# First scale and shift by matmul, constant-tile matmuls, and issue edges round the heads of the first layer

## The chip, the cores and the metric

One core of a Trainium2 chip. The metric is the device time of one launch in microseconds (us), lower is better. Engines: TensorE (PE, with its weight loads as PEld), VectorE (DVE), ScalarE (ACT), GpSimd (POOL), SyncE (SP, which here only issues loads). Each engine works through its own instructions strictly in order.

## The reference, cut to what matters

Four layers over T = 512 rows of width D = 1024: gated linear attention (GLA), a gated convolution MLP, a retention layer, a latent attention layer. The change lies in the first, GLA:

```
cs = silu(c)
shift, scale, gate = split(cs @ mod_w + mod_b, 3)       # 1024 each
h = x * (1 + scale) + shift
q, k, v, r, a = split(h @ gla_w_in)    # 4 heads: q, k 128 wide, v, r 256 wide; a 16 wide
log_a = log_sigmoid(a @ w_a2 + b_a) / 16;  bcum = cumsum(log_a) by chunk
q_dec = q * 128**-0.5 * exp(bcum);  k_inv = k * exp(-bcum)
att = tril(q_dec @ k_inv.T)
o = att @ v + q_dec @ S;  S = S * decay + k_dec.T @ v   # S carried from chunk to chunk
y = (rms_norm(o) * silu(r)) @ gla_w_o
```

## The kernel before, in words

All products run in a form of float32 that TensorE takes in one pass after rounding. To keep the precision each operand is split into a rounded part (`hi`, a cast on ScalarE) and its rest (`lo`, a subtraction on VectorE), and `mm3` does three matmuls: hi by hi, hi by lo, lo by hi (L154 to L156). So every weight tile goes through a load into `raw` (four buffers), a cast (L114) and a subtraction (L115) into `wsp`.

`gla_start` walks the eight 128-row blocks k of the contraction. For each it loads 1 MB of modulation weights (`ms`, in two halves), the block of x transposed (`xq`) and 512 KB of weights (`raw`). VectorE multiplies each `ms` half by the broadcast silu(c) (`csr`) and sums the row (L508): this is scale and shift for the block. ScalarE applies them (L516, into `hT` and `xv`), and 24 matmuls of 512 columns follow, into eight accumulators: v of the first two heads, and q and k of heads 0 and 1.

Then come, on TensorE: 16 matmuls for `a` (L574), the projection r of heads 0 and 1 with the four decay-log matmuls (L601) inside, the transposes of small vectors (L342), then the heads. For each head `gla_prep` makes `qd` and `ki`; `gla_inner` does q by k (12 matmuls of 128 columns), transposes k, splits it into `kt` (L114, L115), masks (`af`), and builds the carried state `sf` by chunk; `gla_outer` gives the output. Between the heads lie the projections q, k of heads 2 and 3 (`gla_qk`), after them v of heads 2 and 3 (`gla_v`), the transposes of the gated output (`gate_T`, L442, split by L117 and L118 into `uT`) and r of heads 2 and 3.

All PSUM banks that are not accumulators come from one pool called `aux`; a matmul into one waits for the readers of what was there. The modulation for the next layer is made by VectorE in sixteen 1024-wide products (L411) of `rawm` tiles, which share the four `raw` buffers. `PLACE` says how many pairs of them are written at each of seven places; a scheduler then interleaves the streams of each engine by its own estimate of when each instruction can start. So the order in the source is not the order on an engine.

Of the kernel before, what the change touches and what calls it, by code (L numbers as in the profile page):

```python
# [67 lines left out]
def layouts(ins):  # L68


    w = ins["gla_w_in"][0]

    def mod(i):
        m, b = ins["mod_w"][0, i], ins["mod_b"][0, i]
        both = np.concatenate([m[:, 1024:2048].T, m[:, 0:1024].T], 1)
        bias = np.stack([b[1024:2048].reshape(8, P), b[0:1024].reshape(8, P)], -1)
        return np.ascontiguousarray(both), np.ascontiguousarray(bias.transpose(1, 0, 2).reshape(P, 16))

    m0, m1 = mod(0), mod(1)
    return {"l_ba": np.ascontiguousarray(ins["gla_b_a"][0].reshape(4, P).T),  # L80
            "l_x": np.ascontiguousarray(ins["x"][0].T),
            "l_mod": m0[0], "l_modb": m0[1], "l_mod1": m1[0], "l_modb1": m1[1],
            "l_c": np.ascontiguousarray(ins["c"].reshape(8, P).T),
            "l_w": np.ascontiguousarray(np.concatenate([w[:, 1024:1536], w[:, 0:256], w[:, 512:768]], 1))}


# [10 lines left out]
class Kern:  # L97
# [125 lines left out]
    def small(self, n, name, dt=F32):  # L223
        return self.tiny.tile([P, 8], dt, tag=name, name=name)[:, :n]

    def rsqrt(self, v):

        nc, n = self.nc, v.shape[1]
        y, t, h = self.small(n, "rs_y"), self.small(n, "rs_t"), self.small(n, "rs_h")
        i = self.small(n, "rs_i", I32)  # L230
        nc.vector.tensor_scalar(i, v.bitcast(I32), 1, None, op0=OP.logical_shift_right)
        nc.vector.tensor_scalar(y.bitcast(I32), i, -1, 0x5F3759DF, op0=OP.mult, op1=OP.add)
        nc.vector.tensor_scalar_mul(h, v, -0.5)
        for _ in range(3):
# [75 lines left out]
    def setup_late(self, ph):  # L310

        nc, a = self.nc, self.a
        self.cs = self.cons.tile([P, 8], F32, name="cs")
        nc.sync.dma_start(self.cs, a["l_c"])
        nc.scalar.activation(self.cs, self.cs, AF.Silu)

    def vectors(self, ph):

# [63 lines left out]
    def gla(self):  # L382
        nc, a, tc = self.nc, self.a, self.tc
        w = a["gla_w_in"][0]
        with ExitStack() as ctx:
# [4 lines left out]
            with tc.tile_pool(name="gla_in", bufs=1, reuse_waits="tile") as ph:  # L390
# [9 lines left out]
                order = list(range(8)) + [(0, 2048), (0, 2560)]  # L400

                def place(where):
                    for _ in range(self.PLACE[where]):
# [12 lines left out]
                decay = self.gla_decay(ph, out, arow)  # L416
                place(0)
                self.gla_r(xT, 0, lambda b, ps: nc.scalar.activation(u[0][:, b, :], ps, AF.Silu))
                place(1)
                self.vectors(ph)  # L420
                tril = out.tile([P, P], F32, name="tril")
                nc.sync.dma_start(tril, a["k_tril"])
                place(2)
            with tc.tile_pool(name="gla_core", bufs=1, reuse_waits="tile") as ph:
# [59 lines left out]
    def gla_start(self, ph, out):  # L484
# [2 lines left out]
        nc, a = self.nc, self.a  # L487
        tl, xT = self.new_hT()
        accs = [self.acc() for _ in range(8)]
        mb = ph.tile([P, 8, 2], F32, name="mb")  # L490
        nc.sync.dma_start(mb, a["l_modb"].rearrange("p (k j) -> p k j", j=2))
        xs = [self.main.tile([P, 2, T], F32, tag=f"res{q}", name=f"xq{q}") for q in range(4)]

        def loads(k):
            r = slice(k * P, k * P + P)
            m = ph.tile([P, 2, D], F32, tag="ms", name="ms", bufs=4)
# [24 lines left out]
            self.split(sp[:, 0], sp[:, 1], raw)  # L521
            return sp

        for k in range(8):
            m, raw = loads(k)
            operand(k, m)
            sp = weights(raw)
            wv = [sp[:, i, 0:512] for i in range(2)]
            for b in range(NB):
                self.mm3(accs[b], [t[:, b * P:(b + 1) * P] for t in xT.k[k]], wv, k == 0, k == 7)  # L530
            for j in range(4):
                self.mm3(accs[4 + j], [sp[:, i, 512 + j * P:640 + j * P] for i in range(2)], xT.k[k], k == 0, k == 7)
# [4 lines left out]
        for h in range(2):  # L537
# [4 lines left out]
        self.setup_late(ph)  # L542
        return xT, v, raws

    def gla_v(self, out, xT, pr):
# [35 lines left out]
    def gla_decay(self, ph, out, a3):  # L581
# [4 lines left out]
        w3, wh, wl, keep = wr[:96, 0], wr[:96, 1], wf[:96, 0], wf[:, 1]  # L586
# [10 lines left out]
        la = ph.tile([P, 4, T], F32, tag="ms", name="la", bufs=self.MS)  # L597
        e = ph.tile([P, 4, T], F32, tag="ms", name="lz", bufs=self.MS)
        for h in range(4):
            pz = self.aux()  # L600
            nc.tensor.matmul(pz, w3[:, h * P:(h + 1) * P], a3, start=True, stop=True)  # L601
            nc.scalar.activation(e[:, h], pz, AF.Abs, bias=ba[:, h:h + 1])
            nc.vector.tensor_scalar(la[:, h], pz, ba[:, h:h + 1], 0.0, op0=OP.add, op1=OP.min)
        nc.scalar.activation(e, e, AF.Exp, scale=-1.0)
        nc.scalar.activation(e, e, AF.Ln, bias=1.0)
        decay = []
        for h in range(4):
            nc.vector.tensor_sub(la[:, h], la[:, h], e[:, h])
            c = ph.tile([P, T], F32, tag="t2", name="cum", bufs=2)
            nc.vector.tensor_tensor_scan(c, keep, la[:, h], 0.0, op0=OP.mult, op1=OP.add)  # L610

            em = self.small(4, "em")
            nc.scalar.activation(em, c[:, 63:T:P], AF.Exp, scale=1.0 / 16)
            d = e[:, h].rearrange("p (b i) -> p b i", b=NB)
            c3 = c.rearrange("p (b i) -> p b i", b=NB)
            nc.vector.tensor_sub(d, c3, c3[:, :, 63:64].to_broadcast([P, NB, P]))
            e1 = out.tile([P, T], F32, name=f"ep{h}")
            e2 = out.tile([P, T], F32, name=f"em{h}")
            nc.scalar.activation(e1, e[:, h], AF.Exp, scale=1.0 / 16)
            nc.scalar.activation(e2, e[:, h], AF.Exp, scale=-1.0 / 16)  # L620

            dk = out.tile([P, 4], F32, name=f"dk{h}")
            nc.vector.tensor_mul(dk[:, 0:3], e1[:, 127:384:P], em[:, 1:4])
            decay.append((e1, e2, dk))
        return decay

    def gla_prep(self, ph, decay, raw):

# [11 lines left out]
    def gla_inner(self, ph, prep, v, tril):  # L640
# [18 lines left out]
        st, sf = [], ph.tile([P, 256], F32, tag="sf", name="sf")  # L659
# [650 lines left out]
```

## Time and profile before

| | |
|---|---|
| time, median of 3 runs (lowest to highest) | 1259.92 us (1258.68 to 1263.08) |
| the profiled execution | 1261.78 us, of which span 1260.0 us |
| TensorE busy | 1225.5 us (97%) |
| VectorE, ScalarE busy | 817.6 us (65%), 535.3 us (42%) |
| mean granted clock of TensorE | 0.994 |
| read from memory | 141.09 MB |

The span is the stretch from the first to the last recorded instruction; the time of a launch has about 1.8 us round it. The granted clock is the share of full speed that TensorE was allowed: 1.00 is 2.4 GHz, 0.50 is 1.2 GHz.

### The profile page before, as it was taken

Reading aid. Unit: us, or ns where it says so; the run is one execution under the profiler, and the core shown is the slowest. Engines: PE = TensorE matmul, PEld = TensorE weight load, DVE = VectorE, ACT = ScalarE, POOL = GpSimd, SP = SyncE. Lnnn points to the kernel's source line nnn. Section 1 sums busy time; section 2 is a strip of 40 time slices with the busy share of each in tenths; the row PEclk is TensorE's granted clock in tenths of the full one; section 3 lists DMA queues with packets and bytes.
Section 4 is the critical chain, followed back from the end, with each engine's and each line's share of the span. In section 5 each row is a group of like instructions: output and inputs, shape, how many; then the busy total and the mean of one; then the engine's idle time right before and its main releaser. Section 6 shows DMA issues by size and latency. Waiting matters only on the chain.

```text
span 1260.0 us, 16047 instructions
## 1 busy us (share of the span) xinstructions
PE 1225.5 (97%) x5982; PEld 1024.9 (81%) x5982; DVE 817.6 (65%) x1836; ACT 535.3 (42%) x946; POOL 3.7 (0%) x15
## 2 busy tenths in 40 slices
PE   5989999999999999999999999999999999999997
PEld 4767877898888888888788888888888888888886
DVE  5698877788442354445875649556454689687755
ACT  3583444533332223341543333433434347577631
POOL 0000000000000000000000000000000000000000
PEclk9998999999999999999999999999999999999999
DMA  9658554147322333333152332323332333212221
GB/s 346 213 171 258 168 195 134 51 125 226 97 90 98 101 99 89 97 134 117 66 158 86 88 90 82 92 85 92 117 106 96 109 98 107 69 50 78 84 84 68
DMA packets 133043, 148.44 MB, mean 118 GB/s; under 512 B 9825, under 2 KB 92152, under 8 KB 132964
## 3 DMA queue, kind: packets, MB, share of 16 engines
q1 hardware_dynamic: 132964, 147.40, 36.5%
q8 instruction: 47, 0.77, 0.3%
q14 instruction: 32, 0.26, 0.1%
HBM read 141.09 MB, written 6.29 MB: 117 GB/s over the span
## 4 chain that ended last, share of the span: by engine, by line
PE 86%; DVE 7%; ACT 4%; DMA 2%; issue 2%; SPq 0%; DVEq 0%; ACTq 0%
PE acc L154 25%; PE acc L156 25%; PE acc L155 25%; PE po L154 1%; PE po L156 1%; PE po L155 1%; PE aux L154 1%; PE aux L156 1%; PE aux L155 1%; DMA raw<-in_gla_w_in 1%; DVE wsp L115 1%; PE aux L899 1%; DMA ms<-in_l_mod 1%; ACT wsp L114 1%; PE aux L1251 1%
## 5 line engine op out<-in xcount | busy, mean ns | idle before, releaser
L115 DVE TENSOR_TENSOR wsp<-raw,wsp 128x1024 fp32r<-128x1024 f32 (+1 forms) x162 | 195.5, 1208 | 192.4 <-ACT wsp L114 192.1
L114 ACT CAST wsp<-raw 128x1024 fp32r<-128x1024 f32 (+1 forms) x162 | 167.9, 1039 | 289.5 <-PE acc L156 253.6
L154 PE MATMUL acc<-hT,wsp 128*128 128x512 f32 (+1 forms) x640 | 244.8, 382 | 0.5 <-DVE v L115 0.5
L156 PE MATMUL acc<-hT,wsp 128*128 128x512 f32 (+1 forms) x640 | 243.7, 381 | 0.0
L155 PE MATMUL acc<-hT,wsp 128*128 128x512 f32 (+1 forms) x640 | 243.3, 380 | 0.0
L154 PE MATMUL acc<-wsp,hT 128*128 128x512 f32 (+2 forms) x448 | 170.0, 386 | 14.6 <-ACT wsp L114 14.6
L155 PE MATMUL acc<-wsp,hT 128*128 128x512 f32 (+2 forms) x448 | 171.6, 383 | 0.0
L156 PE MATMUL acc<-wsp,hT 128*128 128x512 f32 (+2 forms) x448 | 170.3, 382 | 0.0
L154 PEld LDWEIGHTS acc<-hT,wsp 128*128 128x128 f32 x640 | 121.2, 189 | 23.7 <-DVE v L115 1.4
L155 PEld LDWEIGHTS acc<-hT,wsp 128*128 128x128 f32 x640 | 120.9, 189 | 22.1 <-issue 0.2
L156 PEld LDWEIGHTS acc<-hT,wsp 128*128 128x128 f32 x640 | 120.8, 189 | 22.0
L154 PEld LDWEIGHTS acc<-wsp,hT 128*128 128x128 f32 x448 | 84.7, 189 | 29.9 <-ACT wsp L114 14.6
L156 PEld LDWEIGHTS acc<-wsp,hT 128*128 128x128 f32 x448 | 84.6, 189 | 15.1
L155 PEld LDWEIGHTS acc<-wsp,hT 128*128 128x128 f32 x448 | 84.7, 189 | 14.4 <-DVE wsp L115 0.3
L154 PE MATMUL acc<-wsp,uT 128*128 128x512 f32 (+1 forms) x192 | 75.3, 392 | 0.0
L156 PE MATMUL acc<-wsp,uT 128*128 128x512 f32 (+1 forms) x192 | 75.2, 392 | 0.0
L155 PE MATMUL acc<-wsp,uT 128*128 128x512 f32 (+1 forms) x192 | 74.9, 390 | 0.0
L154 PE MATMUL acc<-wsp,p 128*128 128x512 f32 x144 | 56.9, 395 | 0.0
L155 PE MATMUL acc<-wsp,p 128*128 128x512 f32 x144 | 56.9, 395 | 0.0
L156 PE MATMUL acc<-wsp,p 128*128 128x512 f32 x144 | 56.9, 395 | 0.0
L801 DVE SCALAR_TENSOR_TENSOR cv<-acc,cols,cv 128x511 f32<-128x511 f32 x22 | 16.5, 749 | 57.7 <-ACT cv L800 57.7
L800 ACT ACTIVATE cv<-acc,cols 128x512 f32<-128x512 f32 x22 | 17.2, 780 | 82.4 <-PE acc L156 82.4
(357 smaller groups left out, 2062.1 us busy)
## 6 DMA issues: line engine op xcount, KB each, us to landing
raw<-in_w_in_a SPq DMA_DIRECT2D x48, 512.0 KB
raw<-in_ffn_w_up SPq DMA_DIRECT2D x44, 512.0 KB
raw<-in_ffn_w_down SPq DMA_DIRECT2D x22, 512.0 KB
ms<-in_l_mod SPq DMA_DIRECT2D x16, 512.0 KB
raw<-in_gla_w_in SPq DMA_DIRECT2D x16, 512.0 KB
rawm<-in_l_mod SPq DMA_DIRECT2D x16, 512.0 KB
rawm<-in_mod_w SPq DMA_DIRECT2D x16, 512.0 KB
raw<-in_w_out_a SPq DMA_DIRECT2D x16, 512.0 KB
```

The lines of the kernel that those rows point to most:

```text
L114: nc.scalar.copy(hi, src)
L115: nc.vector.tensor_sub(lo, src, self.f(hi))
L154: mm(out, l[0], r[0], start=first, stop=False)
L155: mm(out, l[0], r[1], start=False, stop=False)
L156: mm(out, l[1], r[0], start=False, stop=last)
L800: nc.scalar.activation(t, p, AF.Identity, scale=cw[2 * NT + j], bias=cb[j])
L801: nc.vector.scalar_tensor_tensor(t[:, 1:], p[:, :T - 1], cw[NT + j], t[:, 1:], op0=OP.mult, op1=OP.add)
L899: nc.tensor.transpose(pu[:, b * P:(b + 1) * P], u[:, b, i * P:(i + 1) * P], self.ident)
L1251: nc.tensor.matmul(sc[:, :n], qrT[i][:, s], kr[i][:, :n], start=False, stop=i == 1)
```

## The change

In `gla_start` a new function `first` does block k = 0; the loop does k = 1 to 7 as before. The 1 MB of modulation columns for block 0 comes in a layout of its own (`l_f0`, 256 KB in each of four loads), and scale and shift are 16 matmuls of one column each on TensorE (L546), against silu(c) as eight columns, which one transpose of the small tile `cb` gives. `busy` issues matmuls on a constant tile between them. The load of `csr` moves behind those of block 0. The 24 matmuls of block 0 run with all hi-by-hi products first.

Round the heads: r of heads 0 and 1 is cut after 24 matmuls, where the decay logs stand now; the sums of the decays are made for heads 0 and 1 first (`gla_sums`), for heads 2 and 3 behind head 0; the exponentials run in halves; the state update is one scaled copy on ScalarE and one fused operation on VectorE, rather than an addition and a product on VectorE. `after(engine)` ties what is traced inside it behind the last instruction of that engine, on that engine. `PLACE` changes, and the products of the last three places are tied behind VectorE's last instruction.

```
-    PLACE = (0, 2, 0, 2, 2, 2, 2)
+    WARM = (3, 1, 4, 6)
+    PLACE = (0, 2, 0, 0, 3, 3, 2)
+    def after(self, engine):
+        ins = next(i for i in reversed(self.nc.cur_bb.bb.instructions) if i.engine == engine.engine)
+        return self.tc.issue_after(ins)
...
                 def place(where):
+                    if where > 2:
+                        with self.after(nc.vector):
+                            return place_now(where)
+                    place_now(where)
...
-                decay = self.gla_decay(ph, out, arow)
+                self.vectors(ph)
+                accs = [self.acc() for _ in range(NB)]
+                self.proj_t(xT, self.wsubs(wi, 2048, 2560, 0, 2), 512, None, accs=accs)
+                with self.after(nc.tensor):
+                    logs = self.gla_decay(ph, out, arow)
+                with tc.high_priority():
+                    decay = [self.gla_sums(ph, out, logs, h) for h in range(2)]
                 place(0)
-                self.gla_r(xT, 0, lambda b, ps: nc.scalar.activation(u[0][:, b, :], ps, AF.Silu))
+                self.proj_t(xT, ((k + 2, t) for k, t in self.wsubs(wi, 2048, 2560, 2, 8)), 512,
+                            lambda b, ps: nc.scalar.activation(u[0][:, b, :], ps, AF.Silu), accs=accs)
                 place(1)
-                self.vectors(ph)
...
-                p0 = prep(0)
-                p1 = prep(1)
-                place(3)
-                i0 = self.gla_inner(ph, p0, vh(0), tril)
+                with tc.high_priority():
+                    p0, p1 = prep(0), prep(1)
+                with self.after(nc.tensor):
+                    i0 = self.gla_inner(ph, p0, vh(0), tril)
+                with self.after(nc.scalar), self.after(nc.vector):
+                    decay += [self.gla_sums(ph, out, logs, h) for h in range(2, 4)]
+                    place(3)
...
+            busy(self.WARM[0])
+            with self.after(nc.tensor):
+                nc.tensor.transpose(pt, cb, self.ident[:24, :24])
+                nc.scalar.activation(self.cs, pt[:, 0:8], AF.Silu)
+                nc.vector.tensor_copy(mb.rearrange("p k j -> p (k j)"), pt[:, 8:24])
+            for k in range(8):
+                with self.after(nc.tensor):
+                    if k % 2 == 0:
+                        busy(self.WARM[1 if k else 2])
+                with self.after(nc.tensor):
+                    for j in range(2):
+                        nc.tensor.matmul(pm[j], m[:, k, j], self.cs[:, k:k + 1], start=k == 0, stop=k == 7)
+            with self.after(nc.tensor):
+                busy(self.WARM[3])
...
             if b > 0:
-                nc.vector.tensor_add(sf, pS, sf)
-            nc.vector.tensor_scalar_mul(sf, sf if b else pS, dk[:, b:b + 1])
+                sd = ph.tile([P, 256], F32, tag="sf", name="sd", bufs=3)
+                nc.scalar.activation(sd, sf, AF.Copy, scale=dk[:, b:b + 1])
+                sf = ph.tile([P, 256], F32, tag="sf", name="sf", bufs=3)
+                nc.vector.scalar_tensor_tensor(sf, pS, dk[:, b:b + 1], sd, op0=OP.mult, op1=OP.add)
+            else:
+                nc.vector.tensor_scalar_mul(sf, pS, dk[:, 0:1])
```

The order on the engines follows from the scheduler, so it is shown at three places. First TensorE at the start of the program; `warm` is the constant tile, `m` the modulation columns of block 0. Before:

```order
L154 MATMUL acc<-wsp,hT 128x512 x4
L154 MATMUL acc<-hT,wsp 128x512
L155 MATMUL acc<-wsp,hT 128x512
L156 MATMUL acc<-wsp,hT 128x512
L155 MATMUL acc<-wsp,hT 128x512
```

Now:

```order
L513 MATMUL acc<-warm 128x512 x3
L537 MATMUL acc<-ident,cb 128x24
L513 MATMUL acc<-warm 128x512 x4
L546 MATMUL acc<-cs,m_106 128x1 x4
L513 MATMUL acc<-warm 128x512
L546 MATMUL acc<-cs,m_106 128x1 x4
L513 MATMUL acc<-warm 128x512
L546 MATMUL acc<-cs,m_106 128x1 x4
L513 MATMUL acc<-warm 128x512
L546 MATMUL acc<-cs,m_106 128x1 x4
L513 MATMUL acc<-warm 128x512 x6
L571 MATMUL acc<-wsp,hT 128x512 x4
```

Sixteen constant-tile matmuls, a transpose and 16 one-column matmuls stand ahead of the first product of block 0.

Second ScalarE between `qd` of head 0 and `kt` of head 0; `u` is silu of r. Before:

```order
L418 ACT_TABLE_LOAD
L418 ACTIVATE u_465<-acc 128x512 x4
L114 CAST qd<-qk_449 128x512
L114 CAST ki<-qk_449 128x512
L114 CAST qd<-qk_452 128x512
L114 CAST ki<-qk_452 128x512
L114 CAST kt<-aux 128x384
```

Now:

```order
L116 CAST qd<-qk_491 128x512
L116 CAST ki<-qk_491 128x512
L707 ACTIVATE em_606<-em_606 128x512
L116 CAST qd<-qk_494 128x512
L433 ACT_TABLE_LOAD
L433 ACTIVATE u_504<-acc 128x512
L116 CAST ki<-qk_494 128x512
L433 ACTIVATE u_504<-acc 128x512 x3
L116 CAST wsp<-raw 128x1024 x2
L116 CAST kt<-aux 128x384
```

`qd` and `ki` of head 0 moved ahead of the table load and of `u`; `kt`, which stood behind four casts of 512 columns, stands behind these and two weight casts.

Third VectorE from the split of v of heads 2 and 3 to `kt` of head 2; L417 is the product that was L411, L120 the split of `uT` that was L118. Before:

```order
L115 TENSOR_TENSOR v<-acc,v 128x512
L118 SCALAR_TENSOR_TENSOR uT_73<-aux,cols_714,uT_73 128x512 x4
L115 TENSOR_TENSOR wsp<-raw,wsp 128x1024
L657 TENSOR_TENSOR af<-aux,tril 128x512
L115 TENSOR_TENSOR kt<-aux,kt 128x384
```

Now:

```order
L417 SCALAR_TENSOR_TENSOR rawm,mc_501<-rawm,csr 128x1024 x4
L120 SCALAR_TENSOR_TENSOR uT_73<-aux,cols_533,uT_73 128x512
L417 SCALAR_TENSOR_TENSOR rawm,mc_501<-rawm,csr 128x1024 x2
L120 SCALAR_TENSOR_TENSOR uT_73<-aux,cols_533,uT_73 128x512 x3
L117 TENSOR_TENSOR kt<-aux,kt 128x384
```

Four products stand between the last split of v (just ahead of this piece) and the first of `uT`, and two more behind it. The last two take buffers that the first two give back.

## Rows read from the trace of the kernel before

**Rows 1.** The page, its part on engines: busy us (share of the span) and number of instructions.

```profile
PE 1225.5 (97%) x5982; PEld 1024.9 (81%) x5982; DVE 817.6 (65%) x1836; ACT 535.3 (42%) x946; POOL 3.7 (0%) x15
```

**Rows 2.** The waits of the matmul engine in the first 250 us: who waits, tile and line, for which engine's instruction; us in total, times, longest.

```profile
PE acc L154 <- ACT wsp L114: 14.6, 1, 14.6
PE aux L154 <- ACT ki L114: 4.2, 1, 4.2
PE aux L154 <- ACT kt L114: 2.6, 1, 2.6
PE aux L154 <- DVE sf L665: 0.7, 1, 0.7
...
PE aux L154 <- DVE af L657: 0.5, 1, 0.5
PE aux L601 <- DVE a L578: 0.4, 1, 0.4
```

**Rows 3.** The timeline of all engines at the start: start us, duration us, engine, line, operation, out<-in, in brackets the idle time ahead and what ended it. SPq is SyncE's queue, which issues the loads.

```profile
9.21 1.23 DVE L508 SCALAR_TENSOR_TENSOR ms<-ms,csr 128x1024 f32<-128x1024 f32 x1 [9.21 <-DMA ms<-in_l_mod]
...
12.06 0.81 ACT L516 ACTIVATE hT<-xq,mc 128x512 fp32r<-128x512 f32 x1 [5.59 <-DVE mc L511]
...
13.48 1.03 ACT L114 CAST wsp<-raw 128x1024 fp32r<-128x1024 f32 x1
...
14.56 2.08 PE L154 MATMUL acc<-wsp,hT 128*128 128x512 f32 x4 [14.56 <-ACT wsp L114]
```

**Rows 4.** The timeline of the matmul engine over the first k steps. One matmul is 512 columns wide; the starts tell the pace.

```profile
16.87 0.63 PE L155 MATMUL acc<-wsp,hT 128*128 128x512 f32 x1
17.29 0.63 PE L156 MATMUL acc<-wsp,hT 128*128 128x512 f32 x1
...
20.00 0.39 PE L156 MATMUL acc<-hT,wsp 128*128 128x512 f32 x1
20.23 0.39 PE L154 MATMUL acc<-hT,wsp 128*128 128x512 f32 x1
...
22.27 1.07 PE L154 MATMUL acc<-wsp,hT 128*128 128x512 f32 x4
...
27.71 1.07 PE L154 MATMUL acc<-wsp,hT 128*128 128x512 f32 x4
```

**Rows 5.** One-microsecond stretches of the start: bounds, length, busy us (count) of PE, PEld, DVE, ACT, POOL, granted clock, busy share of the transfer engines, GB/s.

```profile
3.00:4.00 1.00, 0.00 (x0) 0.00 (x0) 0.00 (x0) 0.00 (x0) 0.00 (x0) 1.00 0.82 152
...
10.00:11.00 1.00, 0.00 (x0) 0.00 (x0) 0.96 (x4) 0.00 (x0) 0.00 (x0) 1.00 1.05 426
```

**Rows 6.** The timeline of ScalarE between the decay logs and head 0.

```profile
67.47 2.42 ACT L602 ACTIVATE lz<-aux,ba 128x512 f32<-128x512 f32 x4 [0.80 <-PE aux L601]
69.91 1.28 ACT L604 ACT_TABLE_LOAD   x1
...
74.44 1.92 ACT L605 ACTIVATE lz<-lz 128x2048 f32<-128x2048 f32 x1
...
87.56 1.28 ACT L418 ACT_TABLE_LOAD   x1
88.86 2.06 ACT L418 ACTIVATE u<-acc 128x512 f32<-128x512 f32 x4
...
91.29 0.65 ACT L114 CAST ki<-qk 128x512 fp32r<-128x512 f32 x1
```

**Rows 7.** The timeline of VectorE over the same stretch.

```profile
77.60 2.33 DVE L610 TENSOR_TENSOR_SCAN cum<-wf,la 128x512 f32<-128x512 f32 x2
...
84.65 1.27 DVE L616 TENSOR_TENSOR lz<-cum 128x512 f32<-128x512 f32 x2
...
88.39 1.22 DVE L411 SCALAR_TENSOR_TENSOR rawm<-rawm,csr 128x1024 f32<-128x1024 f32 x1
```

**Rows 8.** The timeline of the matmul engine: its first matmul on head 0 and its first state product of head 1.

```profile
91.99 0.48 PE L154 MATMUL aux<-qd,ki 128*128 128x128 f32 x1 [4.15 <-ACT ki L114]
...
114.35 0.38 PE L154 MATMUL aux<-v,kt 128*128 128x256 f32 x1 [2.55 <-ACT kt L114]
```

**Rows 9.** One-microsecond stretches behind these two waits, columns as in rows 5.

```profile
96.00:97.00 1.00, 1.00 (x5) 0.93 (x5) 0.81 (x2) 0.66 (x1) 0.00 (x0) 0.50 1.15 359
97.00:98.00 1.00, 1.00 (x7) 0.97 (x6) 0.52 (x2) 0.62 (x1) 0.00 (x0) 0.68 0.99 367
...
114.00:115.00 1.00, 0.65 (x4) 0.66 (x5) 1.00 (x3) 1.00 (x3) 0.00 (x0) 0.86 0.97 346
...
117.00:118.00 1.00, 1.00 (x4) 0.81 (x4) 1.00 (x2) 0.41 (x1) 0.00 (x0) 0.50 0.86 303
```

**Rows 10.** The timeline of the matmul engine from the end of the second v projection.

```profile
153.87 0.39 PE L156 MATMUL acc<-wsp,hT 128*128 128x512 f32 x1
154.10 1.91 PE L442 MATMUL aux<-ident,u 128*128 128x128 f32 x16
...
156.50 0.33 PE L154 MATMUL aux<-qd,ki 128*128 128x128 f32 x1
...
158.98 0.39 PE L154 MATMUL aux<-v,kt 128*128 128x256 f32 x1
```

**Rows 11.** The timeline of VectorE over the same stretch.

```profile
155.10 0.69 DVE L115 TENSOR_TENSOR v<-acc,v 128x512 fp32r<-128x512 f32 x1
155.70 2.72 DVE L118 SCALAR_TENSOR_TENSOR uT<-aux,cols,uT 128x512 fp32r<-128x512 f32 x4
```

More of the change, by code (lines that the diff above doesn't have):

```diff
@@ L297, in setup @@
         nc, a = self.nc, self.a
-        cr = a["c"][0]
         self.csr = self.mod.tile([P, D], F32, name="csr")
-        nc.sync.dma_start(self.csr, bass.AP(tensor=cr.tensor, offset=cr.offset, ap=[[0, P], [1, D]]))
-        nc.scalar.activation(self.csr, self.csr, AF.Silu)
+        self.cs = self.cons.tile([P, 8], F32, name="cs")
         self.ident = self.cons.tile([P, P], F32, name="ident")
@@ L308, in setup @@
         self.col = {}
[L310 to L315, printed above, removed]
     def vectors(self, ph):
@@ L489, in gla_start, with busy, first @@
         accs = [self.acc() for _ in range(8)]
+        warm = ph.tile([P, T], F32R, tag="t2", name="warm", bufs=2)
+        nc.vector.tensor_copy(warm, self.ones[:, 0:1].to_broadcast([P, T]))
+        def busy(n):
+            for _ in range(n):
+                nc.tensor.matmul(accs[7], warm[:, :P], warm, start=True, stop=True)
         mb = ph.tile([P, 8, 2], F32, name="mb")
-        nc.sync.dma_start(mb, a["l_modb"].rearrange("p (k j) -> p k j", j=2))
         xs = [self.main.tile([P, 2, T], F32, tag=f"res{q}", name=f"xq{q}") for q in range(4)]
+        def first():
+            cb = ph.tile([24, P], F32, name="cb")
+            nc.scalar.dma_start(cb, a["l_cb"])
+            m = ph.tile([P, 8, 2, P], F32, tag="ms", name="m0", bufs=self.MS)
+            f0 = a["l_f0"].rearrange("p (k j f) -> p k j f", k=8, j=2)
+            raw = self.main.tile([P, self.WN], F32, tag="raw", name="raw", bufs=self.RAW)
+            for k in range(0, 8, 2):
+                nc.sync.dma_start(m[:, k:k + 2], f0[:, k:k + 2])
+            nc.sync.dma_start(xs[0][:, 0], a["l_x"][0:P])
+            halves = [slice(0, 512), slice(512, D)]
+            for h in halves:
+                nc.sync.dma_start(raw[:, h], a["l_w"][0:P, h])
+            cr = a["c"][0]
+            nc.sync.dma_start(self.csr, bass.AP(tensor=cr.tensor, offset=cr.offset, ap=[[0, P], [1, D]]))
+            pt = accs[4][:, 0:24]
+            pm = [accs[6 - j][:, 0:1] for j in range(2)]
+            busy(self.WARM[0])
[12 more added lines that the diff above has]
+                busy(self.WARM[3])
+            mc = self.small(2, "mc")
+            nc.vector.tensor_scalar(mc[:, 0:1], pm[0], mb[:, 0, 0:1], 1.0, op0=OP.add, op1=OP.add)
+            nc.vector.tensor_add(mc[:, 1:2], pm[1], mb[:, 0, 1:2])
+            hi, lo = tl[0][:, 0, 0, :], tl[0][:, 1, 0, :]
+            sp = self.main.tile([P, 2, self.WN], F32R, tag="wsp", name="wsp", bufs=self.WSP)
+            v = ph.tile([P, T], F32, tag="t2", name="xv", bufs=2)
+            with self.after(nc.scalar):
+                for h in halves:
+                    nc.scalar.copy(sp[:, 0, h], raw[:, h])
+            with self.after(nc.scalar):
+                nc.scalar.activation(hi, xs[0][:, 0], AF.Identity, scale=mc[:, 0:1], bias=mc[:, 1:2])
+                nc.scalar.activation(v, xs[0][:, 0], AF.Identity, scale=mc[:, 0:1], bias=mc[:, 1:2])
+            with self.after(nc.vector):
+                for h in halves:
+                    nc.vector.tensor_sub(sp[:, 1, h], raw[:, h], self.f(sp[:, 0, h]))
+                nc.vector.tensor_sub(lo, v, self.f(hi))
+            parts = [([t[:, b * P:(b + 1) * P] for t in xT.k[0]], [sp[:, i, 0:512] for i in range(2)]) for b in range(NB)]
+            parts += [([sp[:, i, 512 + j * P:640 + j * P] for i in range(2)], xT.k[0]) for j in range(4)]
+            order = [[(0, 0), (0, 1), (1, 0)]] * NB + [[(0, 0), (1, 0), (0, 1)]] * 4
+            with self.after(nc.tensor):
+                for t in range(3):
+                    for acc, (l, r), o in zip(accs, parts, order):
+                        nc.tensor.matmul(acc, l[o[t][0]], r[o[t][1]], start=t == 0, stop=False)
@@ L522, in weights @@
             return sp
-        for k in range(8):
+        first()
+        with self.after(nc.scalar):
+            nc.scalar.activation(self.csr, self.csr, AF.Silu)
+        for k in range(1, 8):
             m, raw = loads(k)
@@ L585, in gla_decay @@
         wf = ph.tile([P, 4, T], F32, tag="ms", name="wf", bufs=self.MS)
-        w3, wh, wl, keep = wr[:96, 0], wr[:96, 1], wf[:96, 0], wf[:, 1]
+        keep = out.tile([P, T], F32, name="keep")
+        w3, wh, wl = wr[:96, 0], wr[:96, 1], wf[:96, 0]
         for i in range(6):
@@ L596, in gla_decay @@
         nc.gpsimd.memset(keep[:, 0:T:P], 0.0)
-        la = ph.tile([P, 4, T], F32, tag="ms", name="la", bufs=self.MS)
-        e = ph.tile([P, 4, T], F32, tag="ms", name="lz", bufs=self.MS)
+        la, e = ([out.tile([P, 2, T], F32, name=f"{n}{i}") for i in range(2)] for n in ("ep", "em"))
         for h in range(4):
@@ L601, in gla_decay @@
             nc.tensor.matmul(pz, w3[:, h * P:(h + 1) * P], a3, start=True, stop=True)
[L602 to L624, printed above, removed]
@@ L625, in gla_decay, with gla_sums @@
-        return decay
+            nc.scalar.activation(e[h // 2][:, h % 2], pz, AF.Abs, bias=ba[:, h:h + 1])
+            nc.vector.tensor_scalar(la[h // 2][:, h % 2], pz, ba[:, h:h + 1], 0.0, op0=OP.add, op1=OP.min)
+        for t in e:
+            nc.scalar.activation(t, t, AF.Exp, scale=-1.0)
+        for t in e:
+            nc.scalar.activation(t, t, AF.Ln, bias=1.0)
+        return keep, la, e
+    def gla_sums(self, ph, out, logs, h):
+        nc = self.nc
+        keep, la, e = logs
+        la, e = la[h // 2][:, h % 2], e[h // 2][:, h % 2]
+        nc.vector.tensor_sub(la, la, e)
+        c = ph.tile([P, T], F32, tag="t2", name="cum", bufs=2)
+        nc.vector.tensor_tensor_scan(c, keep, la, 0.0, op0=OP.mult, op1=OP.add)
+        em = self.small(4, "em")
+        nc.scalar.activation(em, c[:, 63:T:P], AF.Exp, scale=1.0 / 16)
+        d = e.rearrange("p (b i) -> p b i", b=NB)
+        c3 = c.rearrange("p (b i) -> p b i", b=NB)
+        nc.vector.tensor_sub(d, c3, c3[:, :, 63:64].to_broadcast([P, NB, P]))
+        nc.scalar.activation(la, e, AF.Exp, scale=1.0 / 16)
+        nc.scalar.activation(e, e, AF.Exp, scale=-1.0 / 16)
+        dk = out.tile([P, 4], F32, name=f"dk{h}")
+        nc.vector.tensor_mul(dk[:, 0:3], la[:, 127:384:P], em[:, 1:4])
+        return la, e, dk
@@ L658, in gla_inner @@
         self.split(at[:, 0], at[:, 1], af)
-        st, sf = [], ph.tile([P, 256], F32, tag="sf", name="sf")
+        st, sf = [], ph.tile([P, 256], F32, tag="sf", name="sf", bufs=3)
         for b in range(3):
```

15 lines of the change are left out of this document (9 added, 6 removed).

## The prediction

> **What bounds the kernel now.** I read the page first: TensorE is busy 1225.5 of 1260.0 us [rows 1], so a gain can only come from its 34 idle microseconds, or from stretches in which it runs at its lower clock. The waits of TensorE say where the idle time is [rows 2]: 14.6 us ahead of the first matmul, then 4.2 us for `ki` of head 0, 2.6 us for `kt` of head 1, and 0.7, 0.5 and 0.4 us. All of it lies in the first 170 us. Behind that TensorE has work all the time, so what is saved or lost round the heads goes to the end unchanged. Third come the timelines and clock of these places.
>
> The start. The first matmul is at 14.56, behind a chain of load (9.21), two products and sums on VectorE, scale (12.06) and cast (13.48, 1.03 long) [rows 3]. The matmuls then start 0.42 us apart, later 0.227 us [rows 4]: the first ones run at half the pace. Block k = 1 starts at 22.27 and block 2 at 27.71, 5.44 us for 24 matmuls [rows 4].
>
> Head 0. TensorE waits 4.15 us, to 91.99 [rows 8], and then runs at a granted clock of 0.50, the 1.2 GHz level, up to the stretch 97 to 98 [rows 9]. Some 5.7 us at half pace lose 2.85, so this place costs 7.0. Head 1 in the same way: 2.55 of waiting to 114.35 [rows 8] and half pace from late in 114 to 115 through 117 to 118 [rows 9], 3.3 us, which lose 1.65: together 4.2. With the 0.44 in front of the decay logs these three cost 11.7.
>
> **The change part by part.** *The start.* TensorE gets sixteen constant-tile matmuls and 16 one-column matmuls, all before 12 us, when it had nothing to do; VectorE loses two 1.2 us products. Block 0 needs f0, x and weights, 1.8 MB, which lie ahead of `csr` in the new queue. But block 1 still needs `csr` and its own `ms`, x and weights, and the bytes ahead of its weights are the same 4.2 MB as before. So the place to look at is the landing of the weights of block 1, not block 0. From the landing of the first `ms` half at 9.21 [rows 3], 3.15 MB remain to them; at 410 GB/s, a little under the settled rate [rows 5], that is 7.7 us: 16.9. Early on the rate falls to 152 GB/s for some microseconds [rows 5]; if that came from the small scattered load `mb`, which now is a small one of another shape, they land up to 2 us earlier, at 14.9. I take 16.2. Behind them in the new order come the cast (1.03), `hT` and `xv` (0.75 each), and on VectorE the `lo` of the weights, a product for block 2 (1.15) and the `lo` of `hT` (0.6): 3.9 us, so the eighth matmul of block 1 starts at 20.1 and 17 more at 0.227 end it at 24.0. Before it was 27.71: 3.7 us gained. Ends: 2.8 (late landing, part of block 0 at half pace) to 5.0 (landing at 14.9). Behind it TensorE is the slowest again: 5.44 us a block, against 1.83 MB or 4.5 us of loads, so the gain stays.
>
> *Heads 0 and 1.* The logs start 24 matmuls into r, not 10, so 3.2 us later; the 0.44 wait goes, as `a` is ready. The chain behind them is shorter. Before: four Abs (2.42), table, Exp (1.92 with its table 3.2), Ln (1.92), then sums for four heads, two scan pairs of 2.33 and so on [rows 6, 7], three products of 1.15 from 88.39 ahead of the splits [rows 7], and the table and `u` ahead of `qd` and `ki` on ScalarE [rows 6]. Now only heads 0 and 1 stand in it: one scan pair and one pair of offsets (1.27) go, so do the three products but one, and 3.3 us of table and `u`. I walk it in the old clock: Abs from 69.9 to 72.4, Exp to 75.7, Ln of the first half to 77.9, differences and scans to 81.5, offsets to 82.7, one product to 83.8, `ki` and its `lo` to 87.0. TensorE is through with r and the vectors at 87.1. So the 4.15 us wait shrinks to 0.1.
>
> But `kt` is late next. On ScalarE between `ki` and `kt` of head 0 now stand the table load (1.28), four `u` (2.06), casts of head 1 and two weight casts of 1.03: from 86.0 to 92.9, and `kt` is there at 93.3. TensorE has 12 small matmuls, 3 transposes and 6 of 512 columns, done by 90.5 with a 0.35 wait in it: 2.75 us of waiting. At head 1 the order of VectorE gives another 1.2 for `kt` and 0.9 for `af` and the `lo` of `kt`, behind products of 1.15. Sum 5.3. A wait of 2.55 cost the clock in head 1 before, so I add the 1.6 that it cost: 6.9 against 11.7, 4.8 gained. Ends: 3.5 (both waits cost the clock) and 6.5 (neither does).
>
> *Heads 2 and 3.* Before, VectorE goes from the last split of v (155.10) straight to the four splits of `uT` at 155.70, 0.68 each [rows 11]. TensorE does the 16 transposes (154.10), then q by k of head 2 at 156.50 and the first state product at 158.98 [rows 10]. Now four products of 1.15 stand ahead of the first split of `uT`, so it ends at 155.70 + 4.6 + 0.6 = 160.9. TensorE's q by k goes into the PSUM bank that this split reads, so it waits for it: from 155.9 to 160.9, 5 us. Then two more products (2.3) and a split: 163.8 for the next bank, while the 12 small matmuls need 1.4 us: another 1.5 of waiting. The state product waits for the third split and for `kt`: 164.8, against 158.98, and two matmuls of 512 columns (0.45) fewer are done by then: 6.3. After 5 us of waiting the clock falls as in head 0; much of the slow time lies in the next wait, so 1.2, not 2.85. The `lo` of `kt` adds 0.3. The weights of r of heads 2 and 3 need the four buffers of these products and come late: 0.6. The new state update saves the 0.7 wait for `sf` [rows 2], as VectorE does one operation rather than two. Sum: a loss of 7.8, from 5 (the clock stays and the second wait is hidden) to 10 (full price of the clock, weights later).
>
> The extra table loads (two of 1.28, ScalarE is busy 42% of the time) lie beside TensorE's work; where they are on the path they are counted above. The moved loads of small vectors are ahead of r now; they are some kilobytes, hidden by the 16 matmuls of `a` (3.9 us).
>
> **Sum.** 3.7 + 4.8 - 7.8 = 0.7 faster. The profiled execution took 1261.78, so a like one takes 1261.1. The median of the runs shown is 1.86 under the profiled one, so 1259.2 for the median.
>
> **A rule against the splitting.** Rows first: in the stretch from 10 to 11 us, in which by the queue's order the 256 KB load of x stands between loads of 512 KB, 426 GB/s flow [rows 5]; loads follow each other without a gap. The Trainium skill, "DMA: Bandwidth & Descriptors", section "Bandwidth", says to put 1 MiB or more into a transfer to get three quarters of the peak, and shows a size of 64 KB at 32% of it. By that the four 256 KB pieces would land later than one piece; at half the rate, an estimate between its two figures, f0 comes 2.5 us later and the start gains 1.2, so that the sum is 1.8 slower. The trace disagrees with it for loads that queue up, so the sum is left as it is.
>
> **The rivals.**
> - *Heads 2 and 3 stall little.* If the products that stand ahead of `uT` are done before the last split of v, or the bank that TensorE wants is another, the loss is that of before, near zero. For it: before, such products were done in the idle time of VectorE (65% busy). Against: the order shown, and in-order engines. Then 3.7 + 4.8 = 8.5, with the clock held in head 0 some 10: 1250 to 1251.5. Chance 0.25.
> - *The weights of r come too late.* The last two products wait for loads into buffers that the first two free, and two weight loads wait for these. If each load takes the 4.5 us of a full queue, not 2 to 3, the second weight tile comes 5 us after TensorE wants it, with the clock low again: 0.7 - 5 = 4.3 slower, 1264.2. It decides once a load takes over 4 us from issue to landing. Against it: the queue is nearly empty there. Chance 0.17.
> - *The start gives nothing.* If the loads land no earlier and TensorE is still at half pace in block 0 (24 at 0.42 us from 12.3 end at 22.4, as before), 3.7 is gone: 1262.9. By rows 4 the first 5 us of work were slow; the constant-tile matmuls are 7 us of such work, though with gaps. Chance 0.10.
>
> **How the numbers follow.** My sum has 0.48, the rivals 0.25, 0.17 and 0.10. The sum's terms can miss by some 1.1, 1.5 and 2.5, together 3: 1256 to 1262.5 is its own range. About 0.3%, 3.8 us, is what a measurement of this kernel can tell from no change: faster means under 1256.1, slower over 1263.7. Faster: 0.25 and a tenth from the sum's edge, 0.34. Slower: most of 0.17 and a little of the other two, 0.19. Same: 0.47. The range reaches to the first rival's slower end and the second rival's: 1251.5 to 1264.
>
> **What would show it.** In the profile of the changed kernel: block 2's matmuls start near 24 (right), or at 27 (wrong). TensorE waits near 0.1 for `ki` and 2 to 3 for `kt` of head 0, with a granted clock of 0.50 behind it. At heads 2 and 3 one wait of 5 us for VectorE's `uT` (L120) with four L417 of 1.2 us ahead of it on VectorE. If this wait is under 2 us, the first rival has it, and the time is near 1251. If TensorE waits for `wsp` of r behind it, it is the second. Wrong altogether would be a loss behind 170 us, which I hold for closed.

## The result and the profile after

The changed kernel took 1267.95 us (median of 4 runs, 1264.37 to 1269.43), against 1260.3 for the kernel before: ratio 1.0054, interval 1.0040 to 1.0068. It is slower, by 7 us; I had forecast no change to be told, at 1259.2, with 1264 as the upper end. The first profiled execution was the quickest of the four, 1264.37 us.

The waits of TensorE in its first 260 us (who waits, for whom; us in total, times, longest), which answer to [rows 2]:

```profile
PE aux L156 <- DVE uT L120: 4.9, 1, 4.9
PE aux L156 <- ACT kt L116: 3.6, 2, 2.5
...
PE aux L738 <- DVE uT L120: 1.6, 1, 1.6
PE po L156 <- ACT scr L775: 1.5, 1, 1.5
PE acc L655 <- ACT qk L622: 1.4, 1, 1.4
PE aux L156 <- DVE af L743: 0.6, 1, 0.6
```

The wait for `ki` of head 0 is gone, the two for `uT` are there. The waits for `po` (ScalarE's squares) and of L655 (the matmuls for `a`, which take over an accumulator whose copy ScalarE has not made yet) are new.

The timeline of TensorE at the start, which answers to [rows 3, 4]; L513 are constant-tile matmuls, L546 the one-column ones (each of the 16 leaves two records, so x8 is a group of four), L571 block 0, the last two rows the first matmuls of blocks 1 and 2:

```profile
5.41 1.10 PE L546 MATMUL acc<-cs,m 128*128 128x1 f32 x8
...
7.83 0.95 PE L546 MATMUL acc<-cs,m 128*128 128x1 f32 x8
...
10.37 2.91 PE L513 MATMUL acc<-warm 128*128 128x512 f32 x6
13.07 1.91 PE L571 MATMUL acc<-wsp,hT 128*128 128x512 f32 x4
...
19.87 0.39 PE L156 MATMUL acc<-wsp,hT 128*128 128x512 f32 x1
...
25.31 0.39 PE L156 MATMUL acc<-wsp,hT 128*128 128x512 f32 x1
```

Block 2 starts at 25.31, against 27.71 [rows 4]. The operand that block 0 waits for, `hT`, is made on ScalarE here:

```profile
10.74 0.81 ACT L559 ACTIVATE hT<-xq,mc 128x512 fp32r<-128x512 f32 x1 [1.08 <-DVE mc L551]
```

It is done at 11.55, and block 0 starts 1.5 us later, behind the six constant-tile matmuls. VectorE from the last split of v of heads 2 and 3, against [rows 11]:

```profile
147.40 0.69 DVE L117 TENSOR_TENSOR v<-acc,v 128x512 fp32r<-128x512 f32 x1 [0.67 <-ACT v L116]
148.01 1.22 DVE L417 SCALAR_TENSOR_TENSOR rawm<-rawm,csr 128x1024 f32<-128x1024 f32 x1
...
152.59 0.75 DVE L120 SCALAR_TENSOR_TENSOR uT<-aux,cols,uT 128x512 fp32r<-128x512 f32 x1
...
155.90 1.23 DVE L417 SCALAR_TENSOR_TENSOR rawm<-rawm,csr 128x1024 f32<-128x1024 f32 x1 [1.43 <-DMA rawm<-in_l_mod]
...
157.05 2.06 DVE L120 SCALAR_TENSOR_TENSOR uT<-aux,cols,uT 128x512 fp32r<-128x512 f32 x3
```

Four products (L417) from 148.01 hold the first split back to 152.59, two more the others, the last of them behind a load.

A later trace of the same kernel (e12) caught an execution of 1269.67 us. Cut at two instructions of TensorE, the first matmul for `a` and the first transpose of the gated output, the three executions read, in us:

| | before, 1261.78 | changed, 1264.37 | changed, 1269.67 |
|---|---|---|---|
| start to `a` | 60.35 | 59.54 | 61.81 |
| `a` to the transposes (heads 0 and 1) | 93.75 | 87.04 | 89.97 |
| transposes to the end (heads 2 and 3 and the rest) | 1105.90 | 1116.02 | 1116.12 |

The loss of 10 us from the transposes on is in both; in the slower execution the start loses 1.5 us and the heads gain 3 less. The trace of the kernel before is itself of an execution 1.5 us above that kernel's median, so gains read against its column come out a little high.

### The profile page after: what moved, and what is told of

The parts are those of the page before. It is cut to its first block, busy times and chain, and to the rows that moved or that the text cites. A ratio compares the mean times of both kernels' runs of the same rounds, so it can differ in the third digit from the quotient of the medians.

```text
span 1262.6 us, 16143 instructions
## 1 busy us (share of the span) xinstructions
PE 1234.5 (98%) x6031; PEld 1032.4 (82%) x6031; DVE 815.0 (65%) x1827; ACT 540.6 (43%) x959; POOL 3.8 (0%) x15
## 4 chain that ended last, share of the span: by engine, by line
PE 86%; DVE 7%; ACT 4%; issue 2%; DMA 1%; DVEq 0%; ACTq 0%; POOL 0%; POOLq 0%
PE acc L156 25%; PE acc L158 25%; PE acc L157 25%; PE po L156 1%; PE po L158 1%; PE po L157 1%; PE aux L156 1%; PE aux L157 1%; PE aux L158 1%; DVE wsp L117 1%; ACT wsp L116 1%; DVE rawm L417 1%; PE aux L989 1%; PE acc L513 1%; PE aux L1341 1%
## 5 line engine op out<-in xcount | busy, mean ns | idle before, releaser
L157 PE MATMUL acc<-wsp,hT 128*128 128x512 f32 (+2 forms) x444 | 169.1, 381 | 0.0
L156 PE MATMUL acc<-wsp,hT 128*128 128x512 f32 (+2 forms) x444 | 169.0, 385 | 0.0
L158 PE MATMUL acc<-wsp,hT 128*128 128x512 f32 (+2 forms) x444 | 167.4, 380 | 0.0
L156 PEld LDWEIGHTS acc<-hT,wsp 128*128 128x128 f32 x636 | 119.8, 188 | 23.8 <-DVE v L117 1.4
L158 PEld LDWEIGHTS acc<-hT,wsp 128*128 128x128 f32 x636 | 119.7, 188 | 22.1 <-DVE wsp L117 0.2
L157 PEld LDWEIGHTS acc<-hT,wsp 128*128 128x128 f32 x636 | 119.7, 188 | 21.7 <-issue 0.2
L156 PEld LDWEIGHTS acc<-wsp,hT 128*128 128x128 f32 x444 | 83.9, 189 | 15.0 <-ACT hT L119 1.1
L158 PEld LDWEIGHTS acc<-wsp,hT 128*128 128x128 f32 x444 | 83.3, 188 | 15.1
L157 PEld LDWEIGHTS acc<-wsp,hT 128*128 128x128 f32 x444 | 83.5, 188 | 13.8
```

The lines of the kernel that those rows point to most:

```text
L156: mm(out, l[0], r[0], start=first, stop=False)
L157: mm(out, l[0], r[1], start=False, stop=False)
L158: mm(out, l[1], r[0], start=False, stop=last)
```

## The experiments

**The changed kernel again**, twice, with no edit.

> The changed kernel once more, unchanged, for a second trace. The first trace is of an execution of 1264.4 us, the others took 1267.5 to 1269.4. Theory A (the loss is the same in every execution, the rest is scatter): the same waits of TensorE, 4.9 and 1.6 us for VectorE's split L120, 2.5 and 1.1 for kt, 1.4 for a copy of q and k, 1.5 for ScalarE's squares, within 0.3 us each, and a time of 1264 to 1266. Theory B (an execution differs by whether the clock falls behind the 2.5 us wait of head 0 as it did in the kernel before): the second trace, if it took 1267 or more, shows a granted clock of 0.50 behind 92 us, costing about 3 us there.

Measured: profiled at 1264.65, the three others 1269.48 to 1269.74; the same waits within 0.3 us, and no low clock behind 92 us until that of heads 2 and 3. So theory A holds for the trace, and not for the three others, which are 5 us longer. The next run caught one of these.

> The changed kernel a third time, for a trace of an execution near 1269. If it is one, theory A says that the one-column matmuls take 1.70 us for eight, block 0 starts at 16.07, and the rest of the 5 us lies in a stretch with a granted clock of 0.50 in heads 0 and 1; theory B says all of it lies at the start. If it is one near 1264.5 again, it shows the same start as the first two traces, 13.07.

Measured 1269.67 us. The start, the same instructions as above:

```profile
5.41 1.70 PE L546 MATMUL acc<-cs,m 128*128 128x1 f32 x8
...
13.37 2.91 PE L513 MATMUL acc<-warm 128*128 128x512 f32 x6
16.07 1.66 PE L571 MATMUL acc<-wsp,hT 128*128 128x512 f32 x4
...
27.58 0.39 PE L156 MATMUL acc<-wsp,hT 128*128 128x512 f32 x1
```

A group of four one-column matmuls takes 1.70 rather than 0.95 us, so the chain to scale and shift is 3 us longer, and block 2 starts at 27.58, as before the change. `hT` on ScalarE is later by as much:

```profile
13.74 0.81 ACT L559 ACTIVATE hT<-xq,mc 128x512 fp32r<-128x512 f32 x1 [3.55 <-DVE mc L551]
```

Behind the waits of heads 0 and 1 (stretches of 2 us, columns as in [rows 5]), the clock is as follows, first in this execution, then in the 1264.37 one:

```profile
96.00:98.00 2.00, 2.00 (x7) 1.65 (x7) 1.54 (x3) 0.81 (x2) 0.00 (x0) 0.50 0.95 350
98.00:100.00 2.00, 2.00 (x8) 1.58 (x7) 2.00 (x6) 0.82 (x2) 0.00 (x0) 0.70 0.66 238
...
114.00:116.00 2.00, 2.00 (x6) 1.52 (x6) 1.35 (x3) 1.04 (x2) 0.00 (x0) 0.50 1.01 369
```

```profile
96.00:98.00 2.00, 2.00 (x11) 1.65 (x10) 2.00 (x5) 0.82 (x2) 0.00 (x0) 1.00 0.79 279
98.00:100.00 2.00, 2.00 (x11) 1.65 (x10) 2.00 (x5) 1.86 (x3) 0.00 (x0) 1.00 0.86 311
...
114.00:116.00 2.00, 2.00 (x11) 1.65 (x10) 2.00 (x5) 2.00 (x5) 0.00 (x0) 1.00 0.51 207
```

The wait for `kt` of head 0 is 2.5 us in both, but in the slower execution the granted clock goes to 0.50, the 1.2 GHz level, behind it and again in head 1, and in the quicker one it stays at 1.00. So theory A: 2.3 us at the start, 2.9 in the heads, 5.2 in all.

**The parts apart.** The kernel before with the new start alone (`first`, its loads and constant tiles, nothing else):

> The kernel before with the new start alone (scale and shift of block 0 by matmul, the constant-tile matmuls, the new order of loads). By the trace of the changed kernel block 2 starts at 25.3 and not 27.7, so 2.4 us faster than the kernel before, about 1257.9; the prediction's step said 3.7. Rival: the shift of the heads by 2.4 us changes which loads are late there and the gain is lost: 1260.

Measured 1263.57 us, ratio 1.0024 (1.0014 to 1.0034): slower, both theories miss. Its trace has the slow start (block 0 at 16.07), the L655 wait of 1.5, and 4.8 us for `ki`. Cut as in the table, it is 1.7 behind the kernel before at `a`; the rest of the 2.4 us between the two spans is mostly a wait of 1.2 for `uT`, less a small gain in the heads.

The new order of the heads with the old start:

> The changed kernel with the start of the kernel before (block 0 through VectorE, csr first). If start and heads add up, this is 2.4 us slower than the changed kernel: near 1267 for an execution like the traced one, 1270 at the median. It shows the 4.9 and 1.6 us waits for L120. Rival: the start delays the heads' loads, so that without it the heads lose less: 1262 or lower.

Measured 1265.51 us (1265.37 to 1266.11), ratio 1.0047, with the same 4.9 and 1.6 us waits for `uT`. That is neither near 1267 nor at 1262, so both theories miss. It lies between the two groups of the changed kernel, and its runs stay within 0.8 us.

**Place 5 untied.** These are the last six of the L417 products.

```
-                    if where > 2:
+                    if where > 2 and where != 5:
```

> The changed kernel, but the last six products of the modulation (place 5) are not tied behind VectorE's last instruction; the scheduler then puts them ahead of the second v projection. Theory (these six products hold up the splits of uT, and with them TensorE by 10 us): the two waits for L120 are gone, the clock stays at 1.00 behind v, and the time falls by 7 to 9 us, to 1256 to 1260. Rival (TensorE waits there for something else as well, the weights of r or kt): 2 to 4 us less only. In either case the products now stand in head 1 and can lengthen the wait for its kt by 1 to 2 us.

Measured 1257.93 us (1254.46 to 1260.45), ratio 0.9980 (0.9966 to 0.9994). The median of the changed kernel run beside it is 1269.59, but there three of four executions were slow ones and here five of ten. Like with like the gain is 9.5 us between the two quick traces (1264.37 and 1254.88) and 9.9 between the slow groups. Its waits up to 250 us:

```profile
PE aux L156 <- ACT kt L116: 4.5, 3, 2.5
PE acc L513 <- DVE warm L509: 1.7, 1, 1.7
PE acc L655 <- ACT qk L622: 1.4, 1, 1.4
PE aux L156 <- DVE af L743: 1.1, 2, 0.6
```

The waits for `uT` and for `po` are gone. From the transposes to the end it takes 1106.07, against 1116.02; over all traces with the new heads that stretch is 1105.9 to 1106.9 in the seven with the products untied and 1116.0 to 1116.6 in the five with them tied. So tying the six products is the cause of the loss at heads 2 and 3. The ten runs fall into 254.5 to 256.6 and 259.3 to 260.5 above 1000. The next run was meant to trace one of the slower kind.

> The kernel with place 5 untied once more, for a second trace: half of its executions took 1254.5 to 1256.6, the others 1259.3 to 1260.5. If the trace is of the slower kind, theory A says that block 0 starts at 16 and not at 13.07 (2.4 us lost by block 2) and that the rest lies behind a wait in heads 0 and 1 with a granted clock of 0.50; theory B says that all of the 5 us lie at the start.

It was another quick one, 1255.75 with block 0 at 13.02, so it decides between neither theory. But the clock fell behind its wait for `kt` of head 0, which is 2.5 us too:

```profile
94.00:96.00 2.00, 2.00 (x6) 1.51 (x6) 2.00 (x4) 0.81 (x2) 0.00 (x0) 0.50 0.88 336
96.00:98.00 2.00, 2.00 (x8) 1.59 (x7) 2.00 (x6) 0.82 (x2) 0.00 (x0) 0.66 0.76 242
```

From `a` to the transposes it took 88.65, against 87.50 in the first trace, where the clock stayed up: 1.15 us. So the quick start and the fall of the clock in head 0 do not exclude each other.

The price of place 5 without the new start, from the heads with the old start and place 5 untied by the same edit:

> The new order of the heads with the start of the kernel before, place 5 untied: what the part on heads 0 and 1 and the new state update give by themselves. By the first trace of the changed kernel the heads gain 6.7 us up to the transposes of the gated output, less what the products that now stand in head 1 cost: 1260.2 - 6 = 1254 to 1256. Rival (it needs the new start to gain): 1258 or more. Together with the run of the heads alone with place 5 tied (1265.5) it gives the price of place 5 without the new start; the theory says 9 to 10.

Measured 1255.53 us, ratio 0.9962: 10.0 under the 1265.51 with place 5 tied. The heads alone are worth 4.5 us, against the 1260.03 of the kernel before run beside it.

**The constant tiles**, taken away but one, place 5 untied:

```
-    WARM = (3, 1, 4, 6)
+    WARM = (1, 0, 0, 0)
```

> The kernel with place 5 untied, and without the constant-tile matmuls but one. Two traces of the new start differ: in the changed kernel the one-column matmuls take 0.95 us for eight and block 0 starts at 13.07; in the run with the start alone they take 1.70 and it starts at 16.07, with no gain over the kernel before. Theory (the clock comes up early only in some executions, falls again under the one-column matmuls, and the six constant-tile matmuls at the end then stand 1.5 to 2.7 us in front of block 0): without them block 0 starts at about 12.9 at half pace and block 2 at 25.9, in every execution, so the two groups of times (254 to 257 and 259 to 260.5 above 1000) draw together, median about 1256. Rival (the constant-tile matmuls do pay): block 2 starts later than 26.5, and the time is 1259 or more.

Measured 1255.5 us, four runs from 1255.17 to 1255.64. The median is 2.4 lower and the two groups are one, as the theory said; what goes is the slower group, for the quick executions with these matmuls took no longer (1254.5 to 1256.6). Its start:

```profile
4.41 6.96 PE L546 MATMUL acc<-cs,m 128*128 128x1 f32 x32 [1.36 <-DMA m<-in_l_f]
12.46 2.08 PE L571 MATMUL acc<-wsp,hT 128*128 128x512 f32 x4 [1.10 <-ACT hT L559]
```

Block 0 starts at 12.46 though the one-column matmuls run at the low pace: nothing stands in front of it but the wait for its operand. But the edit also changed the scheduler's order on VectorE. Behind the sums of the decays stood a product (first row, from the run with place 5 untied alone), and now stands the split of a weight tile of r (second row, from this one):

```profile
82.19 1.22 DVE L417 SCALAR_TENSOR_TENSOR rawm<-rawm,csr 128x1024 f32<-128x1024 f32 x1
...
82.11 1.22 DVE L117 TENSOR_TENSOR wsp<-raw,wsp 128x1024 fp32r<-128x1024 f32 x1
```

With it the 2.5 us wait for `kt` of head 0 became two, one of them already in r:

```profile
83.38 0.50 PE L157 MATMUL acc<-wsp,hT 128*128 128x512 f32 x1 [1.80 <-DVE wsp L117]
...
92.57 0.39 PE L156 MATMUL aux<-v,kt 128*128 128x256 f32 x1 [1.11 <-ACT kt L116]
```

`kt` itself comes no earlier (92.57 here, 92.66 there). All five traces with the divided wait (this one, the two with the old start and the new heads, and the two further ones without constant tiles) show a granted clock of 1.00 from 80 to 100 us; of the seven with a whole wait of 2.3 to 2.5 us four show a fall. So the narrowing has two possible causes, the start and the divided wait, and no run separates them.

The same edit with place 5 still tied:

> The changed kernel, place 5 still tied, without the constant-tile matmuls but one. Theory (the products of place 5 cost near 9 to 10 us whatever the start, and the scatter of the changed kernel comes from its start): about 1255.5 + 9.5 = 1265, within 1 us in all executions, so 3 to 5 us under the changed kernel's median, and the two waits for L120 of 4.9 and 1.6 to 1.9 us in the trace. Rival (the scatter of the changed kernel comes from the clock behind the waits at heads 2 and 3): the times still spread over 4 us or more.

Measured 1265.07 us (1264.11 to 1265.45), with 4.9 and 1.5 us of waiting for `uT`: as the theory said, but for a spread of 1.3 rather than 1 us. The 5 us scatter of the changed kernel goes with the constant tiles, by their place in the queue or by the order that they bring about.

**Filling the wait of head 0** with nine matmuls on existing data, place 5 untied:

```
...
+            if b == 0:
+                for _ in range(n):
+                    nc.tensor.matmul(full, fill[:, :P], fill, start=True, stop=True)
```

> The kernel with place 5 untied, and nine matmuls on existing data into the bank of the first state product of head 0, in the 2.5 us wait for kt; the six matmuls of q and k of head 2 move behind the state products. Theory (in the slower executions the clock falls behind this wait): the times at 1259 to 1260.5 vanish or draw nearer to the lower group, median 1256. Rival (the two groups come from the start alone): the two groups stay, 2.5 us or more apart.

Measured 1260.4 us (1257.19 to 1261.13), no gain. Two runs lie at 1257.2 and 1257.8, eight at 1260.0 to 1261.1, so two groups stay. But the trace, of the 1257.19 execution, shows that the wait was not filled:

```profile
87.87 2.33 PE L751 MATMUL aux<-hT 128*128 128x512 f32 x9
92.54 0.39 PE L156 MATMUL aux<-v,kt 128*128 128x256 f32 x1 [2.33 <-ACT kt L116]
...
94.00:96.00 2.00, 2.00 (x7) 1.58 (x7) 2.00 (x5) 0.81 (x2) 0.00 (x0) 0.55 0.95 344
```

The nine matmuls took the place of the six useful ones, which moved behind `kt`; TensorE still waits 2.33 us for it, and the clock falls. The trace is 2.3 us above the quick one without them. So the run tests neither theory.

**The order of the accumulators**, place 5 untied:

```
-            for j in range(4):
+            for j in ((3, 0, 1, 2) if k == 7 else range(4)):
```

> The kernel with place 5 untied, and in block 7 the accumulator that the matmuls for a take over is finished first of its four, so that its copy is the first of four on ScalarE. Theory: the 1.43 us wait of these matmuls (L655) for that copy is gone and all behind it is 1.4 us earlier: median 1256.5. Rival: the chain behind a (decay logs) is bound by ScalarE, whose work is the same, and the wait moves to ki: no change, 1257.9.

Measured 1256.95 us (1255.93 to 1259.6). The L655 wait is gone from the trace, which is of a slow start (block 0 at 16.07, 1257.24 us), and the median is 1.0 lower, within the scatter of the start. Without the constant tiles the same edit is clearer:

> Place 5 untied, no constant-tile matmuls but one, and the accumulator of a finished first. Theory: the 0.7 us wait for the copy of q and k that the trace without the constant tiles has is gone, 1255.5 - 0.7 = 1254.8, in a group as narrow as there (0.5 us). Rival: the time saved is taken up by the wait for kt of head 0, which ScalarE sets: 1255.5.

Measured 1253.92 us (1252.97 to 1254.95), ratio 0.9951 (0.9936 to 0.9965): 1.6 under the 1255.5, and 6 us faster than the kernel before. That is more than the 0.7 forecast, in a group 2 us wide and not 0.5: 0.9 of the 1.7 us that its trace gains up to `a` is there at block 2 (25.12 against 25.98), ahead of the edit. Cut as in the table it reads 57.76, 87.46 and 1105.98: the start gains 2.6 us over the kernel before, the heads 6.3, and nothing is lost behind them. This is the best version of the study, and beats both kernels.

## Why the prediction was wrong

**The start, the step that failed.** I put it at 3.7 gained; it was -1.5 in the 1269.67 execution and 0.8 in the 1264.37 one. My sum let the landing of the weights of block 1 set the pace. What set it was TensorE's own queue.
- The landing was at my favourable end: ScalarE's cast of the weights of block 1 is released by the load at 14.85, where I had bounds of 14.9 and 16.9. But TensorE could not use it. My sum needs block 0 done by 18.5, so from the 12.3 of my third rival at nearly the full pace; it starts at 13.07 or 16.07, runs at half pace up to about 16 or 17.5, and ends at 19.87 or 22.14.
- The cost of the constant-tile matmuls I set at nothing, since TensorE "had nothing to do" before 12 us. The six last ones stand in its queue ahead of block 0 and take 2.7 us at half pace; block 0 starts 1.5 us behind its operand, at 13.07 with `hT` done at 11.55. In the slower execution it is 1.5 us again (14.55 and 16.07). There the other constant-tile matmuls are on the path too: they stand between one-column matmuls at the low pace, which are on the chain to scale and shift, and `hT` starts 2.2 us later than without constant tiles (13.74 against 11.59). In the quick execution it starts 0.9 earlier.
- I did not look for a wait of L655. It costs 1.4 us in the runs with the new start, 0.7 in those without the constant tiles, and the runs with the old start and the new heads do not have it. The new start, not the moved vectors, brings it; finishing the accumulator first takes it away.

"The start gives nothing" stood among the rivals with a chance of 0.10 and a price of 1262.9, for the half pace in block 0. The slower executions give nothing at block 2, but by another mechanism: the half pace lies in the one-column matmuls ahead of block 0, which then takes 6.1 us and not 10. The L655 wait came on top.

**Heads 0 and 1, right.** 4.8 gained was forecast (3.5 to 6.5); from `a` to the transposes it is 6.7 and 3.8. The wait for `ki` went from 4.15 to nothing (0.1 forecast), `kt` of head 0 waits 2.5 (2.75), head 1 another 1.1 and 0.6 (1.2 and 0.9). Whether the clock falls behind the 2.5 us I took as the likelier case, at 1.6; it differs from execution to execution. My ends, neither and both, are about the two traces. The new heads by themselves, with the old start and place 5 untied, are worth 4.5 by the medians.

**Heads 2 and 3, right in kind, low by 2.** Forecast a wait of 5 us and one of 1.5: 4.9, and 1.6 to 2.0. The first state product comes 13.25 us behind the transposes (146.58 to 159.83), where I had 6.3 on top of the 4.88 of [rows 10], plus 1.2 for the clock. The clock stays at its low level from the end of the first wait to about 162, so the three matmuls of 512 columns and the small ones ahead of the state product run at half pace too:

```profile
160.00:162.00 2.00, 2.00 (x11) 1.90 (x10) 0.90 (x3) 1.68 (x3) 0.00 (x0) 0.50 0.88 292
```

From the transposes to the end TensorE waits 11.7 us in all, against 4.5 before; so of the 10.1 us lost 7.2 are waits and 2.9 half pace, where I had 1.2 for the clock. The second product of the last two waited 1.43 us for its load; 1.5 us for `po` I had not listed. Sum forecast 7.8 (its terms add up to 7.7), up to 10; measured 10.1 to the end, and 10.0 by untying place 5 with the old start. My second rival, weights of r too late with TensorE waiting for `wsp`, did not happen.

So the sum was 0.7 faster by +3.7, +4.8, -7.8, and the slower trace says -1.5, +3.8, -10.2: 7.9 slower, which is its 1267.9 us of span against 1260.0. Of the 8.6 us between, 5.2 are the start, 1.0 heads 0 and 1 and 2.4 heads 2 and 3.

## What to carry to other kernels

A filler instruction is free only if nothing useful is queued behind it on its in-order engine: cost it by what stands next in the queue and when that becomes ready, at the clock that the engine has then. Tying work behind the last instruction of an engine moves all of it ahead of what that engine would do next; here six products of 1.2 us ahead of the splits that release a PSUM bank cost 10 us. A median over few runs can hide two groups of times, so compare group with group, and trace more than one execution before a gain of 2 us is put down to a cause. Under a scheduler an edit in one place can change the order in another, so compare the order on every engine before the edit is given the credit.

## What the runs showed that I had not expected

TensorE was busy without a gap and yet lost its clock. In the 1264.37 execution, columns as in [rows 5]:

```profile
8.00:9.00 1.00, 1.00 (x11) 0.96 (x10) 0.00 (x0) 0.60 (x1) 0.00 (x0) 1.00 1.06 424
9.00:10.00 1.00, 1.00 (x8) 1.00 (x6) 0.00 (x0) 0.64 (x2) 0.00 (x0) 0.56 1.04 426
...
15.00:16.00 1.00, 1.00 (x3) 0.77 (x3) 0.88 (x5) 1.00 (x2) 0.00 (x0) 0.52 1.04 414
16.00:17.00 1.00, 1.00 (x6) 0.83 (x5) 1.00 (x1) 1.00 (x2) 0.00 (x0) 1.00 1.01 391
```

One-column matmuls, with one constant-tile matmul between two groups, fill the engine from 5.4 to 10.4; the granted clock falls to 0.56 in the stretch from 9 to 10 and is back at 1.00 in that from 16 to 17, behind constant-tile and real matmuls of 512 columns. Without the constant tiles the one-column matmuls stay at the low pace through all their 6.96 us, and block 0 behind them starts at it (four matmuls from 12.46 to 14.33). In the 1269.67 execution the record says 1.00 throughout the first 20 us while the pace is the low one (1.70 us a group): there the pace, not the record, tells the clock. The Trainium skill, "TensorE: Matmul & The Clock Gate", section "What's actually happening", has the clock low by default and released by activity; the pace at the start of all traces agrees (0.42 us a matmul in [rows 4]). Why the same instructions lift the clock by 5.4 us in one execution and not in another, and keep it or lose it behind the same 2.5 us wait, no run here settles.
